# Score products of dilation 16 read their stationary operand from tiles in residue order

## The chip, the cores and the metric

One NeuronCore of one Trainium2 chip runs the whole program. The time is the device time of one launch in microseconds. The kernel before takes 3086.87 us (median of three runs, 3085.54 to 3091.45).

## The reference

One layer of an encoder on 2048 tokens of width 1024. Two groups of heads run on the same input: eight heads of dilated attention (64 wide) and four heads of a bidirectional mLSTM (128 wide); then an output projection, a gated feed-forward network with a convolution, and a small gated addition. The change touches the attention heads. For each head:

```python
ATTN_PATTERNS = ((128, 1), (512, 4), (2048, 16))      # window, dilation
def dilated_branch(q, k, v, dil, n_side):
    M = S // dil
    def to_res(t):
        return t.reshape(B, H, M, dil, hd).transpose(0, 1, 3, 2, 4)
    o, lse = banded_attention(to_res(q), to_res(k), to_res(v), n_side)
    ...
for window, dil in ATTN_PATTERNS:
    o, l = dilated_branch(q, k, v, dil, (window // 2) // dil)
    outs.append(o)
    lses.append(l)
wts = jax.nn.softmax(jnp.stack(lses, axis=0), axis=0)
out = jnp.sum(wts[..., None] * jnp.stack(outs, axis=0), axis=0)
```

Dilation 16 splits the 2048 tokens into 16 residue classes of 128 tokens, and each token attends within its class. Dilation 4 has four classes of 512 tokens in bands, dilation 1 is a band of tokens in their own order.

## The kernel before, in words

All matrix products of the layer run on TensorE; fp32 operands of the scores are held as a high part and a low part in fp32r, and a score block is two products added in PSUM.

**Layouts.** A head has its keys and queries with the features on the partitions and the 2048 tokens along the free axis. `qs` (queries, high part on partitions 0 to 63, low part on 64 to 127), `ks1` (keys, high part twice) and `ks2` (keys, low part, and a row 64 of ones) come from DRAM in token order (`load`, L858). `km1`, `km2` and `qm1`, `qm2` are the same in residue order: token 16a + r stands at place 128r + a. ACT makes `km1` and DVE makes `km2`, a quarter at a time (`keys_by_residue`, L879); DVE makes `qm1` (`queries_by_residue`, L887), and a DMA copies its upper half to `qm2`. Row 64 of `km2` is zero. Row 64 of `qm2` receives the negative row maximum, through DRAM.

**The two passes.** Pass A (`pass_a`, L936) multiplies queries (stationary) by keys (moving) for all three patterns; DVE takes the row maxima from PSUM (L956). At its end the three maxima are transposed, sent through DRAM, combined, and written to `qm2`. Pass B (`pass_b`, L1046) multiplies keys (stationary) by queries (moving), with the maximum subtracted by the extra row; ACT takes the exponential (L993), GpSimd (POOL) masks the band (L929, L931; DVE in half of the last head's steps), and the products with the values, fp32, follow three steps later (`values`, L1004), added into `oacc` by ACT (dilation 16) or DVE (the others).

**Units.** A pattern has 16 units (`unit`, L895). A unit is one stationary block of 128 tokens and one moving window, read from the tiles in residue order. The stationary block of dilation 1 is 128 neighbouring tokens of a tile in token order, that of dilation 4 every fourth token, that of dilation 16 every sixteenth: `return slice(i, i + 2033, 16), ...`. The moving window of dilation 16 is 128 neighbouring places of a tile in residue order; that of the others has 192 or 256 places.

**Steps and order.** A step of dilation 16 holds four units (eight products), a step of the others two units (four products). Pass A of a head has 21 steps: dilation 16 (4 steps), 1 (8), 4 (8), and the one that combines the maxima. Pass B has 20 score steps, dilation 16 (4), 4 (8), 1 (8), and three that only finish values. `run` (L1079) interleaves: one step of pass B of head h, then one step of the stream of A passes, which is 30 steps ahead at the start (`LEAD`). So beside the first three B steps of a head stand A steps 10 to 12 of the next head, beside B steps 4 to 11 its A steps 13 to 20, beside step 12 its step 21, and beside B steps 13 to 21 the A steps 1 to 9 of the head after it. `stream` (L1082) puts the loads and copies at yields of the A pass: the load of the next head at yield 8, query copies at 9, 11, 13 and 15, key copies of the next head at 14, 16, 18 and 20. Pass A of head 0 and the start of head 1's run beside the last of the input projections (L147 to L149).

**Memory.** The large tiles are pages of a pool of 22 (`NPAGES`), one page each for `qs`, `ks1`, `ks2`, `km1`, `km2`, `qm1`, `qm2`, `oacc` and the three value tiles `vt`. `qs`, `km1` and `km2` are given up at the end of pass A. PSUM has three banks for pass A (`psa`), three for pass B (`psb`), two for values (`pso`).

**Order of the instructions.** Each engine runs its own queue in order. A list scheduler fills the queues: it takes what is ready by priority in program order, and a tile waits until a page is free, so a DMA can be issued ahead of its place in the program. All DMAs of this part go through the queue of SyncE (SP), in order.

Of the kernel before, what the change touches and what calls it, by code (L numbers as in the profile page):

```python
# [11 lines left out]
F32 = mybir.dt.float32  # L12
# [8 lines left out]
P = 128  # L21
# [6 lines left out]
AH = 8  # L28
HD = 64
# [76 lines left out]
def page(g, shape, dtype=F32, name="pg"):  # L106
    n = int(np.prod(shape[1:]))
    return shaped(g.pages.tile([P, PAGE], dtype, name=name, tag="pg")[:shape[0], :n], shape)
# [720 lines left out]
class Attention:  # L829


    def __init__(self, g, pool, psA):
        nc = g.nc
# [34 lines left out]
        def residues(t):  # L868
            return t.rearrange("p (r a) -> p r a", a=P)
# [17 lines left out]
        def queries_by_residue(H, q):  # L887
            if q == 0:
                H.qm1 = page(g, [P, S], F32R, name="qm1")
                H.qm2 = page(g, [65, S], F32R, name="qm2")  # L890
            to_residues(nc.vector, H.qm1, H.qs, q)
            if q == 3:
                nc.sync.dma_start(H.qm2[:64].bitcast(F32), H.qm1[:64].bitcast(F32))

        def unit(p, i):  # L895

            if p == 0:
                lo, hi = max(0, 8 * i - 4), min(P, 8 * i + 12)
                return slice(P * i, P * i + P), (lambda t: residues(t)[:, :, lo:hi]), lo, hi, lo - (8 * i - 4)
            if p == 1:  # L900
                r, j = divmod(i, 4)
                lo, hi = max(0, 32 * j - 16), min(P, 32 * j + 48)
                t0 = r + 512 * j
                return slice(t0, t0 + 509, 4), (lambda t: t.rearrange("p (b r a) -> p r b a", r=4, a=P)[:, r, :, lo:hi]), lo, hi, lo - (32 * j - 16)
            return slice(i, i + 2033, 16), (lambda t: t[:, P * i:P * i + P]), 0, P, 0

        def width(p, lo, hi):
            return OUTER[p] * (hi - lo)
# [1 line left out]
        def shape3(p, ap, lo, hi):  # L910
            return ap if p == 2 else ap.rearrange("p (x y) -> p x y", y=hi - lo)
# [24 lines left out]
        def pass_a(h, H):  # L936

            mst = pool.tile([P, 3, 16], F32, name="mst", tag="mst", bufs=2)
            for p in (2, 0, 1):
                per = 4 if p == 2 else 2  # L940
                W = 512 // per
                for i0 in range(0, 16, per):
                    ps = psA.tile([P, 512], F32, name="psa", tag="psa")
                    for u in range(per):
                        st, win, lo, hi, off = unit(p, i0 + u)
                        o = shape3(p, ps[:, u * W:u * W + width(p, lo, hi)], lo, hi)
                        nc.tensor.matmul(o, lhsT=H.qs[:, st], rhs=win(H.km1), start=True, stop=False)  # L947
                        nc.tensor.matmul(o, lhsT=H.qs[:65, st], rhs=win(H.km2), start=False, stop=True)  # L948
                    for u in range(per):
                        i = i0 + u  # L950
                        st, win, lo, hi, off = unit(p, i)
                        n = width(p, lo, hi)
                        o = shape3(p, ps[:, u * W:u * W + n], lo, hi)
                        junk = pool.tile([P, 256], BF16, name="junk", tag="junk", bufs=1)
                        m = add[p] if p == 2 else add[p][:, :, off:off + hi - lo]
                        nc.vector.tensor_tensor_reduce(shape3(p, junk[:, :n], lo, hi), o, m, 1.0, -3e38, ALU.add, ALU.max, mst[:, p, i:i + 1])  # L956
                    yield
            ps = psA.tile([P, 512], F32, name="psa", tag="psa")
            for p in range(3):
                nc.tensor.transpose(ps[:16, P * p:P * p + P], mst[:, p], g.ident)  # L960
            neg = pool.tile([16, 2, P], F32, name="neg", tag="neg", bufs=1)
            nc.vector.tensor_scalar(neg[:, 0].rearrange("b (r a) -> b r a", r=16), ps[:16, 0:P].rearrange("b (a r) -> b r a", r=16), -1.0, None, ALU.mult)
            nc.vector.tensor_scalar(neg[:, 1].rearrange("b (r a) -> b r a", r=4), ps[:16, P:2 * P].rearrange("b (a r) -> b r a", r=4), -1.0, None, ALU.mult)
            nc.sync.dma_start(g.mx[h, 0].rearrange("r (b a) -> b r a", a=8), neg[:, 0].rearrange("b (r a) -> b r a", r=16))
            for r in range(4):
                nc.sync.dma_start(g.mx[h, 1].rearrange("(b r) (j a) -> r j b a", r=4, a=32)[r], neg[4 * r:4 * r + 4, 1].rearrange("j (b a) -> j b a", b=4))
            x12 = pool.tile([16, 2, P], F32, name="x12", tag="x12", bufs=1)
            nc.sync.dma_start(x12, g.mx[h].rearrange("s r a -> r s a"))
            nc.vector.tensor_tensor(x12[:, 0], x12[:, 0], x12[:, 1], ALU.min)
            mrow = pool.tile([16, P], F32R, name="mrow", tag="mrow", bufs=1)  # L970
            nc.vector.scalar_tensor_tensor(mrow, ps[:16, 2 * P:3 * P], -1.0, x12[:, 0], ALU.mult, ALU.min)
            nc.sync.dma_start(H.qm2[64:65].bitcast(F32).rearrange("o (r a) -> o r a", a=P), mrow.bitcast(F32))
            yield

        def weights(h, H, p, i0):

            per = 4 if p == 2 else 2
            W = 512 // per
            ps = self.psB.tile([P, 512], F32, name="psb", tag="psb")
            if i0 % (2 * per) == 0:  # L980
                H.e2 = raw(g, [P, 2, 512], name="e")
            e = H.e2[:, (i0 // per) % 2]
            us = [unit(p, i0 + u) for u in range(per)]
            widths = [width(p, x[2], x[3]) for x in us]
            for u in range(per):
                st, win, lo, hi, off = us[u]
                o = shape3(p, ps[:, u * W:u * W + widths[u]], lo, hi)
                nc.tensor.matmul(o, lhsT=H.ks1[:, st], rhs=win(H.qm1), start=True, stop=False)
                nc.tensor.matmul(o, lhsT=H.ks2[:, st], rhs=win(H.qm2), start=False, stop=True)  # L989
            for u0, u1 in ([(0, per)] if min(widths) == W else [(u, u + 1) for u in range(per)]):  # L990
                cs = slice(u0 * W, (u1 - 1) * W + widths[u0])
                st, win, lo, hi, off = us[u0]
                nc.scalar.activation(e[:, cs], ps[:, cs], AF.Exp, scale=0.125)  # L993
                if on_dve(h, p, i0 // per):
                    v = e[:, cs] if p == 2 else e[:, cs].rearrange("k (u x y) -> k u x y", u=u1 - u0, x=OUTER[p])
                    for u in range(u1 - u0):
                        if p == 2:
                            o, m = e[:, W * u:W * u + W], add[p]
                        else:
                            o, m = v[:, u], add[p][:, :, off:off + hi - lo]  # L1000
                        nc.vector.scalar_tensor_tensor(o, m, 0.0, o, ALU.is_equal, ALU.mult)
                else:
                    sel(p, e[:, cs], u1 - u0, hi - lo, off)
            return e, us, widths  # L1004
# [41 lines left out]
        def pass_b(h, H):  # L1046
            H.oacc = page(g, [P, S], F32, name="oacc")
            H.banks = {}
            steps = [(2, i) for i in range(0, 16, 4)] + [(p, i) for p in (1, 0) for i in range(0, 16, 2)]
            pend = []  # L1050
            for k, (p, i0) in enumerate(steps):
                pend.append((p, i0, weights(h, H, p, i0)))
                if len(pend) > LOOK:
                    values(h, H, *pend.pop(0))
                yield
            for x in pend:
                values(h, H, *x)
                yield
# [22 lines left out]
        def stream():  # L1081
            for q in range(4):  # L1082
                keys_by_residue(heads[0], q)
            for h in range(AH):
                H = heads[h]
                n = 0
                for _ in pass_a(h, H):
                    n += 1
                    if n == 8 and h + 1 < AH:
                        heads[h + 1] = load(h + 1)  # L1090
                    if n in (9, 11, 13, 15):
                        queries_by_residue(H, (n - 9) // 2)
                    if n in (14, 16, 18, 20) and h + 1 < AH:
                        keys_by_residue(heads[h + 1], (n - 14) // 2)
                    yield
                H.qs = H.km1 = H.km2 = None

        def start():
            heads[0] = load(0)
# [1242 lines left out]
```

## Time and profile before

| | us |
|---|---|
| median of three runs | 3086.87 |
| the profiled execution | 3087.83 |
| its span, first to last instruction | 3086.0 |
| PE busy (matmuls) | 2910.5 (94%) |
| PEld busy (weight loads) | 2481.0 (80%) |
| DVE busy | 2048.7 (66%) |
| ACT busy | 1277.4 (41%) |
| POOL busy | 1072.4 (35%) |

The attention heads run from about 617 to 1100 us of the span. Matmul durations overlap, since matmuls are pipelined: how fast TensorE works is read from the distance between starts. PE is the row of matmuls, PEld that of weight loads, which run ahead of their matmuls. The granted clock is a share of TensorE's full 2.4 GHz.

### The profile page before, as it was taken

To read this page: it belongs to the slowest core of one execution; us is meant where nothing else is said; L and a number is where in the kernel's file an instruction comes from. 1 tells how busy PE (TensorE), PEld (TensorE's weight loads), DVE (VectorE), ACT (ScalarE), POOL (GpSimd) and SP (SyncE) were. 2 spreads that over 40 slices of the span, in tenths; PEclk is the share of its full clock that TensorE was granted. 3 is DMA by queue.
4 is the path that set the end of the run, shared out by engine and by line. 5 is a ranking of instruction groups with operands and counts; after the bars stand their busy time and mean duration, and the time that the engine had idled before them with its cause. 6 is when DMAs were issued, how large, how long until landed. Compare 5 with 4: busy or idle time off the path is not lost.

```text
span 3086.0 us, 41017 instructions
## 1 busy us (share of the span) xinstructions
PE 2910.5 (94%) x14474; PEld 2481.0 (80%) x14474; DVE 2048.7 (66%) x4107; ACT 1277.4 (41%) x2428; POOL 1072.4 (35%) x1146
## 2 busy tenths in 40 slices
PE   8889899899999989799899999799999999999999
PEld 7867887799999978687578887678888777877887
DVE  5866786566656478534977777977777566646444
ACT  5555465433332346323444444444444223223332
POOL 2133423414444546101433332533334141433221
PEclk9999999879899899899899999899999999999999
DMA  7744425464452563556222223222224876765111
GB/s 216 206 137 130 142 95 171 135 159 98 97 122 59 157 202 122 156 166 224 95 82 82 82 78 103 79 82 82 82 82 138 299 266 226 238 211 203 45 43 43
DMA packets 386781, 419.70 MB, mean 136 GB/s; under 512 B 107448, under 2 KB 300856, under 8 KB 380936
## 3 DMA queue, kind: packets, MB, share of 16 engines
q1 hardware_dynamic: 386576, 417.09, 44.4%
q8 instruction: 114, 1.87, 0.3%
q14 instruction: 91, 0.75, 0.1%
HBM read 308.09 MB, written 104.61 MB: 134 GB/s over the span
## 4 chain that ended last, share of the span: by engine, by line
PE 44%; DVE 7%; DMA 5%; POOL 3%; issue 3%; ACT 1%; SPq 1%; POOLq 0%; DVEq 0%; ACTq 0%
PE ps L1806 8%; PE ps L1808 8%; PE ps L1807 8%; PE ps L149 6%; PE ps L147 6%; PE ps L148 5%; DMA ar<-a_d 2%; POOL ar L175 1%; DVE as L176 1%; DVE fw L176 1%; DMA wdr<-in_w_ffn_down_dram 1%; DVE wd L176 1%; DVE bl L176 1%; DVE wdr L175 1%; PE psm L1475 1%
## 5 line engine op out<-in xcount | busy, mean ns | idle before, releaser
L1806 PE MATMUL ps<-bh,fw 128*128 128x512 f32 x1232 | 494.6, 402 | 29.8 <-ACT fw L176 12.0
L1808 PE MATMUL ps<-bh,fw 128*128 128x512 f32 x1232 | 490.8, 399 | 7.5 <-DVE fw L176 7.5
L1807 PE MATMUL ps<-bl,fw 128*128 128x512 f32 x1232 | 491.8, 399 | 4.1 <-DVE bl L176 3.2
L175 POOL TENSOR_TENSOR sum<-fraw 128x512 f32<-128x512 f32 x132 | 197.1, 1493 | 405.9 <-DVE fw L176 359.8
L1806 PEld LDWEIGHTS ps<-bh,fw 128*128 128x128 f32 x1232 | 235.9, 191 | 94.3 <-ACT fw L176 14.2
L1808 PEld LDWEIGHTS ps<-bh,fw 128*128 128x128 f32 x1232 | 235.7, 191 | 64.1 <-DVE fw L176 10.4
L1807 PEld LDWEIGHTS ps<-bl,fw 128*128 128x128 f32 x1232 | 235.9, 191 | 60.5 <-DVE bl L176 7.4
L147 PE MATMUL ps<-wd,as 128*128 128x512 f32 x616 | 244.8, 397 | 14.1 <-ACT as L176 14.1
L149 PE MATMUL ps<-wd,as 128*128 128x512 f32 x616 | 245.4, 398 | 5.9 <-DVE as L176 5.9
L175 POOL TENSOR_TENSOR ar<-ar 128x768 f32<-128x768 f32 x80 | 143.3, 1811 | 294.6 <-DMA ar<-a_d 227.5
L148 PE MATMUL ps<-wd,as 128*128 128x512 f32 x616 | 243.4, 395 | 0.0
L176 ACT ACTIVATE fw<-sum 128x512 fp32r<-128x512 f32 x220 | 134.6, 628 | 241.3 <-DVE sum L175 142.5
L176 DVE TENSOR_TENSOR fw<-sum,fw 128x512 fp32r<-128x512 f32 x220 | 214.1, 988 | 8.0 <-ACT fw L176 7.7
L993 ACT ACTIVATE e<-psb 128x512 f32<-128x512 f32 (+2 forms) x240 | 95.5, 434 | 258.7 <-PE psb L989 248.5
L176 ACT ACTIVATE as<-ar 128x768 fp32r<-128x768 f32 x108 | 85.1, 792 | 271.7 <-POOL ar L175 218.7
L929 POOL TENSOR_SCALAR_AFFINE_SELECT e<-e 128x64 f32<-128x64 f32 (+2 forms) x225 | 98.4, 437 | 245.3 <-ACT e L993 238.7
L176 DVE TENSOR_TENSOR as<-ar,as 128x768 fp32r<-128x768 f32 x108 | 110.3, 1029 | 109.6 <-ACT as L176 109.3
L956 DVE CUSTOM_DVE_ANT_0 junk<-psa,mask 128x256 bf16<-128x256 f32 (+1 forms) x304 | 111.1, 365 | 86.8 <-PE psa L948 78.7
L1879 POOL TENSOR_TENSOR act<-act,up 128x512 f32<-128x512 f32 x88 | 129.2, 1468 | 87.9 <-DVE up L1828 68.8
L947 PE MATMUL psa<-km,qs 128*128 128x256 f32 (+2 forms) x384 | 150.4, 397 | 4.8 <-ACT km L875 4.8
L147 PEld LDWEIGHTS ps<-wd,as 128*128 128x128 f32 x616 | 117.0, 190 | 42.2 <-ACT as L176 16.6
L1870 DVE SCALAR_TENSOR_TENSOR act<-ext,fcw,act 128x512 f32<-128x512 f32 (+1 forms) x176 | 136.4, 815 | 16.7 <-ACT act L1868 16.1
(351 smaller groups left out, 7829.7 us busy)
## 6 DMA issues: line engine op xcount, KB each, us to landing
ar<-a_d SPq DMA_DIRECT2D x94, 384.0 KB
ar<-a_d SPq DMA_DIRECT2D x94, 320.0 KB
wdr<-in_w_ffn_down_dram SPq DMA_DIRECT2D x50, 512.0 KB
fraw<-in_w_ffn_gate_dram SPq DMA_DIRECT2D x22, 1024.0 KB
fraw<-in_w_ffn_up_dram SPq DMA_DIRECT2D x22, 1024.0 KB
a_d<-act SPq DMA_DIRECT2D x88, 256.0 KB
xT_d<-xT SPq DMA_DIRECT2D x32, 512.0 KB
bx<-xT_d SPq DMA_DIRECT2D x16, 1024.0 KB
```

Of the source, the lines that this page charges most:

```text
L147: g.nc.tensor.matmul(out, lhsT=sh, rhs=mh, start=start, stop=False)
L148: g.nc.tensor.matmul(out, lhsT=sh, rhs=ml, start=False, stop=False)
L149: g.nc.tensor.matmul(out, lhsT=sl, rhs=mh, start=False, stop=stop)
L175: eng[0].tensor_tensor(src, a, b, ALU.add if sign > 0 else ALU.subtract)
L176: return (lambda: g.nc.scalar.activation(hi, src, AF.Copy)), (lambda: eng[1].tensor_tensor(lo, src, hi.bitcast(F32), ALU.subtract))
L947: nc.tensor.matmul(o, lhsT=H.qs[:, st], rhs=win(H.km1), start=True, stop=False)
L956: nc.vector.tensor_tensor_reduce(shape3(p, junk[:, :n], lo, hi), o, m, 1.0, -3e38, ALU.add, ALU.max, mst[:, p, i:i + 1])
L1806: nc.tensor.matmul(ps, lhsT=w[:, 0, k], rhs=h[:, k], start=start and k == 0, stop=False, skip_group_check=True)
L1807: nc.tensor.matmul(ps, lhsT=w[:, 0, k], rhs=l[:, k], start=False, stop=False, skip_group_check=True)
L1808: nc.tensor.matmul(ps, lhsT=w[:, 1, k], rhs=h[:, k], start=False, stop=k == 3, skip_group_check=True)
L1870: nc.vector.scalar_tensor_tensor(act, ext[a][:, lo + k:hi + k], self.cw[:, k, f:f + 1], act, ALU.mult, ALU.add)
L1879: nc.gpsimd.tensor_tensor(act, act, up[a][:, lo:hi], ALU.mult)
```

## The change

Units of dilation 16 take their stationary block from the tile in residue order, where its 128 tokens are neighbours: `qm1` in place of `qs` in pass A, `km1` and `km2` in place of `ks1` and `ks2` in pass B. For that

- `unit` returns a function that cuts the block out of a tile, in place of a slice;
- pass A takes the patterns in the order of dilation 1, 4, 16, and its query copies come two yields earlier (7, 9, 11, 13), the load of the next head two yields later (10);
- `km1` and `km2` are kept until the fourth step of pass B, and at the end of pass A a DMA writes the row of ones into row 64 of `km2`, which pass A needs as zeros.

```diff
@@ unit
             if p == 0:
...
-                return slice(P * i, P * i + P), (lambda t: residues(t)[:, :, lo:hi]), lo, hi, lo - (8 * i - 4)
+                return (lambda t: t[:, P * i:P * i + P]), (lambda t: residues(t)[:, :, lo:hi]), lo, hi, lo - (8 * i - 4)
             if p == 1:
...
-                return slice(t0, t0 + 509, 4), (lambda t: t.rearrange("p (b r a) -> p r b a", r=4, a=P)[:, r, :, lo:hi]), lo, hi, lo - (32 * j - 16)
-            return slice(i, i + 2033, 16), (lambda t: t[:, P * i:P * i + P]), 0, P, 0
+                return (lambda t: t[:, t0:t0 + 509:4]), (lambda t: t.rearrange("p (b r a) -> p r b a", r=4, a=P)[:, r, :, lo:hi]), lo, hi, lo - (32 * j - 16)
+            return (lambda t: t[:, P * i:P * i + P]), (lambda t: t[:, P * i:P * i + P]), 0, P, 0
@@ pass_a
-            for p in (2, 0, 1):
+            for p in (0, 1, 2):
...
-                        nc.tensor.matmul(o, lhsT=H.qs[:, st], rhs=win(H.km1), start=True, stop=False)
-                        nc.tensor.matmul(o, lhsT=H.qs[:65, st], rhs=win(H.km2), start=False, stop=True)
+                        q = st(H.qm1 if p == 2 else H.qs)
+                        nc.tensor.matmul(o, lhsT=q, rhs=win(H.km1), start=True, stop=False)
+                        nc.tensor.matmul(o, lhsT=q[:65], rhs=win(H.km2), start=False, stop=True)
...
             nc.sync.dma_start(H.qm2[64:65].bitcast(F32).rearrange("o (r a) -> o r a", a=P), mrow.bitcast(F32))
+            nc.sync.dma_start(H.km2[64:65].bitcast(F32), g.kl[h, HD:HD + 1])
@@ weights
-                nc.tensor.matmul(o, lhsT=H.ks1[:, st], rhs=win(H.qm1), start=True, stop=False)
-                nc.tensor.matmul(o, lhsT=H.ks2[:, st], rhs=win(H.qm2), start=False, stop=True)
+                nc.tensor.matmul(o, lhsT=st(H.km1 if p == 2 else H.ks1), rhs=win(H.qm1), start=True, stop=False)
+                nc.tensor.matmul(o, lhsT=st(H.km2 if p == 2 else H.ks2), rhs=win(H.qm2), start=False, stop=True)
@@ pass_b
                 pend.append((p, i0, weights(h, H, p, i0)))
+                if p == 2 and i0 == 12:
+                    H.km1 = H.km2 = None
@@ stream
-                    if n == 8 and h + 1 < AH:
+                    if n == 10 and h + 1 < AH:
                         heads[h + 1] = load(h + 1)
-                    if n in (9, 11, 13, 15):
-                        queries_by_residue(H, (n - 9) // 2)
+                    if n in (7, 9, 11, 13):
+                        queries_by_residue(H, (n - 7) // 2)
...
-                H.qs = H.km1 = H.km2 = None
+                H.qs = None
```

## Rows read from the trace of the kernel before

**Rows 1.** The page, part 1: busy time, share of the span, instructions.
```profile
PE 2910.5 (94%) x14474; PEld 2481.0 (80%) x14474; DVE 2048.7 (66%) x4107; ACT 1277.4 (41%) x2428; POOL 1072.4 (35%) x1146
```

**Rows 2.** Busy time by stretch, one head: length, engines, clock, DMA share, GB/s.
```profile
779.00:833.70 54.70, 54.70 (x306) 53.82 (x304) 33.45 (x119) 17.88 (x38) 25.16 (x61) 0.94 0.49 108
```

**Rows 3.** Waits in that head: engine, line, releaser, total us, times, longest.
```profile
ACT e L993 <- PE psb L989: 35.4, 18, 5.8
DVE junk L956 <- PE psa L948: 16.1, 15, 1.7
```

**Rows 4.** Timeline of PE, an A step: start us, us, engine, line, tiles.
```profile
757.23 0.42 PE L947 MATMUL psa<-km,qs 128*128 128x128 f32 x1
...
758.80 0.39 PE L948 MATMUL psa<-km,qs 65*128 65x128 f32 x1
759.02 0.34 PE L988 MATMUL psb<-qm,ks 128*128 128x256 f32 x1
...
759.56 0.92 PE L1034 MATMUL pso<-e,vt 128*128 128x192 f32 x4
```

**Rows 5.** Timeline of PE, a B step of dilation 16.
```profile
726.28 0.33 PE L988 MATMUL psb<-qm,ks 128*128 128x128 f32 x1
...
727.99 0.34 PE L947 MATMUL psa<-km,qs 128*128 128x256 f32 x1
```

**Rows 6.** Timeline of PEld, values loads, then an A step of dilation 4.
```profile
739.14 0.99 PEld L1014 LDWEIGHTS pso<-e,vt 128*128 128x128 f32 x8
740.05 0.31 PEld L947 LDWEIGHTS psa<-km,qs 128*128 128x128 f32 x1
...
740.97 0.33 PEld L988 LDWEIGHTS psb<-qm,ks 128*128 128x128 f32 x1
```

**Rows 7.** Timeline of PE, products of dilation 1 with 192 columns.
```profile
719.20 0.25 PE L988 MATMUL psb<-qm,ks 128*128 128x192 f32 x1
719.29 0.28 PE L989 MATMUL psb<-qm,ks 65*128 65x192 f32 x1
719.40 0.35 PE L1034 MATMUL pso<-e,vt 128*128 128x64 f32 x2
```

**Rows 8.** Busy time by stretch, around the first B steps of head 1.
```profile
724.20:729.10 4.90, 4.90 (x28) 4.90 (x28) 1.91 (x7) 1.19 (x2) 1.04 (x3) 1.00 0.49 109
729.10:735.90 6.80, 6.80 (x32) 6.80 (x33) 4.26 (x12) 2.17 (x4) 4.45 (x7) 0.50 0.32 75
```

**Rows 9.** Busy time by stretch, pass B of head 7.
```profile
1055.00:1092.00 37.00, 32.83 (x180) 29.84 (x180) 21.47 (x47) 16.30 (x46) 17.07 (x32) 0.88 0.25 54
```

**Rows 10.** Busy time by stretch, the start of head 0.
```profile
616.50:633.50 17.00, 15.81 (x70) 15.53 (x71) 10.83 (x51) 7.13 (x10) 0.58 (x1) 0.50 0.93 209
```

**Rows 11.** Timeline of all engines, the start of head 0.
```profile
616.58 3.97 ACT L875 ACTIVATE km<-ks 128x512 fp32r<-128x512 f32 x4 [7.55 <-DMA ks<-qk_d]
617.69 0.48 PE L947 MATMUL psa<-km,qs 128*128 128x128 f32 x1 [4.80 <-ACT km L875]
...
619.85 2.20 DVE L877 CAST km<-ks 64x512 fp32r<-64x512 f32 x4
...
621.97 0.31 PE L948 MATMUL psa<-km,qs 65*128 65x128 f32 x1
```

**Rows 12.** Timeline of SP's queue: loads of head 4, maxima of head 2.
```profile
741.10 0.55 SPq L863 DMA_DIRECT2D qs<-qk_d  x1
...
758.93 1.38 SPq L865 DMA_DIRECT2D ks<-kl_d  x1
...
767.89 0.56 SPq L972 DMA_DIRECT2D qm<-mrow  x1
```

**Rows 13.** Timeline of DVE and ACT: key copies of head 4.
```profile
786.88 2.83 DVE L877 CAST km<-ks 64x512 fp32r<-64x512 f32 x2
790.13 4.07 ACT L875 ACTIVATE km<-ks 128x512 fp32r<-128x512 f32 x4
```

**Rows 14.** Busy time by stretch, the highest DMA rate.
```profile
600.00:620.00 20.00, 15.20 (x117) 14.71 (x115) 8.77 (x27) 7.84 (x17) 9.43 (x12) 0.91 0.95 229
```

## The prediction

> **What bounds the kernel now.** I read the page's busy shares first: the TensorE matmuls (PE) cover 94% of the span, its weight loads 80%, DVE 66% [rows 1]. The change touches attention alone, so the shares of that stretch count. In one full head of the steady state (779.0 to 833.7 us) PE is busy for all 54.70 us, DVE for 33.45, ACT for 17.88, POOL for 25.16 [rows 2]. The waits of that head name only engines that wait for PE: ACT 35.4 us, DVE 16.1 us; no wait of PE is listed [rows 3]. So PE's own instruction spacing is the period of a head, and I read that spacing from the starts in the timeline, not from the durations, which overlap.
>
> In an A step of dilation 16 (eight products of 128 columns) the starts run from 757.23 to 758.80, and the next line starts at 759.02: 1.79 us, or 0.22 us per product. The four products after it, of 256 columns each with a contiguous stationary operand, take from 759.02 to 759.56, 0.135 us each [rows 4]. Twice the columns in less time: the 0.22 us is not set by the moving columns. A B step of dilation 16 is the same: 726.28 to 727.99, 1.71 us [rows 5]. What the two have in common is the stationary operand, read at every 16th element.
>
> **What a contiguous load would cost.** No row shows a 128-column fp32r product with a contiguous stationary operand, so I bound it. Eight weight loads of 128 contiguous columns for 128 moving columns (the values products) run from 739.14 to 740.05: 0.114 us each [rows 6]. Score products with 192 columns and a contiguous operand start at 719.20, 719.29 and are followed at 719.40: 0.09 and 0.11 us [rows 7]. From below 0.09, from above 0.22 (no gain). I take 0.11, nearest to both rows: 0.88 us for a step of eight, a gain of 0.91 us in an A step and 0.83 us in a B step. At 0.09 a step would gain another 0.16 us.
>
> The Trainium skill ("TensorE: Matmul & The Clock Gate", LDWEIGHTS) says that a weight load takes its columns divided by 1.2, in ns, and nothing else: 107 ns for 128. The contiguous loads agree with it (0.114 us), the loads of dilation 16 do not (0.22 us). By that rule alone an order in memory changes nothing, and the time stays; that is the fourth case below.
>
> **The change, part by part.**
>
> *A steps, heads 1 to 7.* 7 x 4 steps at 0.91 us: 25.5 us less. All of it lies on PE, which sets the period [rows 2].
>
> *B steps, heads 0 to 6.* 28 steps at 0.83 us would be 23.2 us. But the granted clock is 1.00 up to 729.1 us and 0.50 (1.2 instead of 2.4 GHz) from 729.1 to 735.9 [rows 8]. The fall comes 4.9 us after the first B step of the head, in the stretch where no values products run yet. At half clock a contiguous product doubles to about 0.22 us, and gains nothing. In the changed order the first B steps stand beside A steps of dilation 4, 0.92 us each (740.05 to 740.97) [rows 6]; a pair is then 0.88 + 0.92 = 1.80 us, so 2.7 of the four B steps come ahead of the fall, and 1.3 gain nothing. 7 x 2.7 x 0.83 = 15.7 us less. Whether the clock still falls no row can tell, since the stretch gets shorter (three pairs of 1.80 instead of 2.25 us) and denser; I keep the fall here and make its absence a rival.
>
> *B steps, head 7.* Here the scan of the other mixer runs alongside and PE is busy for only 32.83 of 37.00 us [rows 9]. Between nothing and 4 x 0.83 = 3.3 us less; I take half, 1.7.
>
> *A pass of head 0.* It begins at 617.7 us, and the clock is at 0.50 from 616.5 to 633.5 [rows 10]. Now its dilation-16 steps stand in that stretch; after the change its dilation-1 steps do, which double there (8 steps of four products, 0.11 us more each: 3.5 us), while the dilation-16 steps move out of it and gain 4 x 0.91 = 3.6. The two cancel; 0, bounds plus and minus 3.
>
> *The order of the A pass.* The first step of dilation 16 needs a quarter of the keys in residue order, a step of dilation 1 needs all of them. Later heads have them early. In head 0 ACT's four copies run from 616.58 for 3.97 us, and PE, idle before, takes its first product at 617.69; DVE's four end near 622, and PE's first L948 product already waits until 621.97 [rows 11]. So at most 620.55 - 617.69 = 2.9 us more, at least 0 if projection products are placed ahead; I take 1.5 us more.
>
> *Queries earlier, load later.* The casts of the queries are the same, two steps sooner: nothing on PE. The five loads of the next head move from yield 8 to yield 10 of an A pass, its key copies stay at yields 14 to 20. In the trace the loads of head 4 are issued from 741.10 to 758.93 us, its first key casts run at 786.88 (DVE) and 790.13 (ACT) [rows 12, 13]: 28 us of cover, of which the shift and the pages held longer take a part. Nothing as long as it lasts; the price without it is in the slower case.
>
> *Keys held longer, row of ones.* km1 and km2 stay in their two pages of 22 until the fourth B step, some 15 steps more. One more DMA per head of a row of 8 KB goes on SP's queue behind the maximum row (767.89 us for head 2) [rows 12], and is read by the first B step, 11 us later (779). The maximum row itself waits longer than the products that the new DMA waits for, so nothing new waits, and what is queued behind it (a chunk of the values load) moves by its 0.56 us of issue. 0.
>
> The sum: 25.5 + 15.7 + 1.7 - 1.5 = 41.4 us. The profiled execution took 3087.8 us (span 3086.0 and 1.8 around it), 0.9 above the median of the three, 3086.9. So 3087.8 - 41.4 = 3046.4, and against the median 3045.
>
> What is late next: with 6 us less per head, DVE stands at 33.45 of some 49 us, and still waits for PE.
>
> **The rivals.**
>
> 1. *The clock no longer falls* in the denser stretch. For it: the dilation-16 stretch is the only one of a head in which it falls. Against it: three steps without values products remain. Then the 1.3 steps of seven heads gain too (7.6 us), and the half-clock time itself goes: the eight values products of a step double in it from 0.91 us [rows 6], and some score products with them, so about 1.2 us per head, 8.5 us. 3045 - 16 = 3029.
>
> 2. *Another engine takes over for part of the head.* DVE's and ACT's order near the first B steps is dense, since the key copies of the head after next (2.83 us on DVE, 4.07 us on ACT [rows 13]) and the output product fall there; faster steps bring them nearer. If half the gain is lost: 3066. Against it: both engines idle for over a third of the head [rows 2].
>
> 3. *Slower: pages and late loads.* The loads of a head come only when three pages are free. With km1 and km2 held and the load at yield 10, four steps (some 8 us) are left to the key copies, if the loads are not issued ahead of their place as they are now. A head's five loads are 2.5 MB; the best rate of a stretch, 229 GB/s [rows 14], makes that 11 us, the mean of a head, 108 GB/s [rows 2], makes it 23 us. ACT and DVE would stand in front of the copies for 3 to 15 us and the exponentials behind them with them. The point from which it decides is 41.4 / 6 = 7 us of PE standing still in each of six heads; at 10 us the time would be 3045 + 60 = 3105. Against it: 28 us of cover now.
>
> 4. *It does nothing.* If the 0.22 us belongs to products of 128 fp32r columns and not to the stride, the steps stay as they are: 3087. For it: no contiguous one is in the trace. Against it: 128 columns in the values products at 0.114 us.
>
> **How the numbers follow.** The forecast has 0.47 (own range 3036 to 3052: the spacing of 0.09 us gives 0.16 x 47 = 7.5 us more, head 0 plus or minus 3, its start 1.5, head 7 1.7). The clock case 0.28, the partly covered one 0.13, no effect 0.06, slower 0.06. A measurement of this kernel tells about 0.2%, 6 us, from no change; so faster 0.88, same 0.06, slower 0.06. For eight in ten I leave out the last two, the worse part of the covered case, and the best of the clock case with 0.09 us: 3022 to 3067.
>
> **What would show it.** In the timeline of the changed kernel the dilation-16 products should start 0.11 us apart, both in A and B steps, and a head should take some 49 us, with PE busy throughout. The clock at half for 7 to 10 us per head, about 5 us after the first B step, is the forecast; a full clock there is rival 1. Waits of PE for ACT or DVE in the B steps of dilation 4, with a DMA of the keys behind them, are rival 3. Products at 0.22 us with contiguous operands are rival 4. The prediction is wrong if the spacing stays above 0.15 us, or if a head's period shrinks by less than 3 us.

## The result, and the profile after

The changed kernel takes 3058.49 us (median of four runs, 3050.90 to 3060.52), the kernel before in the same rounds 3088.36 (3085.54 to 3091.45). The ratio is 0.9899, 95% interval 0.9878 to 0.9919: about 30 us, or 1%, faster. The time lies in the forecast's range (3022 to 3067), but 13.5 us above the forecast itself and outside its own range (3036 to 3052). The profiled execution is one of the longer ones, 3060.42 us.

Most lines of the code move by two to five: what was L947 and L948 is now L949 and L950, L988 and L989 are L991 and L992, L956 is L958.

The page's line of busy times answers to [rows 1]:

```profile
PE 2875.3 (94%) x14474; PEld 2437.7 (80%) x14474; DVE 2032.9 (66%) x4107; ACT 1278.4 (42%) x2428; POOL 1084.5 (35%) x1146
```

PE is 35.2 us shorter with the same 14474 instructions. Busy time by stretch (columns as in [rows 2]): one steady head, then the stretch around its first B steps, then the rest up to the end of the last head:

```profile
770.88:820.35 49.47, 49.47 (x305) 48.47 (x304) 31.59 (x119) 17.91 (x38) 26.81 (x61) 0.93 0.54 119
769.00:773.90 4.90, 4.90 (x34) 4.82 (x32) 2.17 (x8) 1.20 (x2) 1.25 (x4) 1.00 0.49 109
773.90:780.70 6.80, 6.80 (x33) 6.80 (x32) 3.56 (x11) 2.27 (x4) 3.30 (x6) 0.50 0.56 130
1024.79:1061.60 36.81, 32.77 (x179) 29.56 (x178) 20.18 (x44) 13.80 (x39) 15.93 (x31) 0.91 0.23 50
```

A head is 49.47 us long where it was 54.70 [rows 2], and PE is still busy for all of it. The clock still falls to 0.50 for 6.80 us [rows 8], here 4.1 us after the first B step begins (769.78). Over heads 1 to 6 that distance is 4.1 to 5.9 us, and it was 4.1 to 6.4 before; in head 1 of [rows 8] the first B step begins at 723.96, so the fall came 5.1 us after it, not the 4.9 that the prediction reads. In that same head PE waits for nobody; the list of waits answers to [rows 3]:

```profile
ACT e L996 <- PE psb L992: 30.1, 18, 5.5
...
DVE junk L958 <- PE psa L950: 10.3, 12, 1.5
```

The timeline of PE, a B step of dilation 16 ahead of the fall of the clock, and one after it [rows 5]:

```profile
771.73 0.24 PE L991 MATMUL psb<-qm,km 128*128 128x128 f32 x1
771.81 0.27 PE L992 MATMUL psb<-qm,km 65*128 65x128 f32 x1
...
772.59 0.43 PE L949 MATMUL psa<-km,qs 128*128 128x192 f32 x1
...
775.92 0.36 PE L991 MATMUL psb<-qm,km 128*128 128x128 f32 x1
...
777.57 0.73 PE L1017 MATMUL pso<-e,vt 128*128 128x128 f32 x2
```

Eight products take 772.59 - 771.73 = 0.86 us, where they took 1.71; after the fall 777.57 - 775.92 = 1.65, a gain of next to nothing. And an A step, answering to [rows 4]:

```profile
790.08 0.41 PE L949 MATMUL psa<-km,qm 128*128 128x128 f32 x1
...
790.88 0.28 PE L949 MATMUL psa<-km,qm 128*128 128x128 f32 x1
791.00 0.28 PE L950 MATMUL psa<-km,qm 65*128 65x128 f32 x1
791.11 0.43 PE L991 MATMUL psb<-qm,ks 128*128 128x192 f32 x1
```

The starts are 0.11 us apart (791.00 to 791.11), but the step takes 1.03 us, not 0.88: its second product starts 0.25 us after the first (790.33). Summed from each start to the next over all heads, the A products of dilation 16 went from 56.96 to 32.27 us, the B products from 55.02 to 37.12: 42.6 us together.

Two things were given back. The first is waits of PE, at the start of head 0 and at the transposes of the maxima (L962), in heads 0 and 7:

```profile
620.86 1.01 PE L949 MATMUL psa<-km,qs 128*128 128x192 f32 x3 [6.11 <-ACT km L875]
...
655.93 0.38 PE L962 MATMUL psa<-ident,mst 128*16 128x128 f32 x1 [3.50 <-DVE mst L958]
...
1000.66 0.28 PE L962 MATMUL psa<-ident,mst 128*16 128x128 f32 x1 [1.97 <-DVE mst L958]
```

The first was 4.80 us before [rows 11], the other two were not there. All waits of PE from 616 us to the end of the last head sum to 17.3 us, where they were 9.3: 8.0 us more. So the last head ends at 1061.6 instead of 1096.8 us, 35.2 us earlier. The second is no part of the change: from there to the end the program is the same, yet took 1997.0 us in this profile and 1989.2 in that of before.

The loads have less cover. The last load of head 4 in SP's queue, and the first key cast on DVE, with the last key cast and the query casts:

```profile
764.87 0.34 SPq L865 DMA_DIRECT2D ks<-kl_d  x1
```

```profile
776.91 0.60 DVE L877 CAST km<-ks 64x512 fp32r<-64x512 f32 x1
...
785.37 0.63 DVE L877 CAST km<-ks 64x512 fp32r<-64x512 f32 x1
785.91 2.22 DVE L877 CAST qm<-qs 128x512 fp32r<-128x512 f32 x4
```

776.91 - 764.87 = 12 us, where it was 28 [rows 12, 13].

### The profile page after: what moved, and what is told of

The parts are those of the page before. It is cut to its first block, busy times and chain, and to the rows that moved or that the text cites. A ratio compares the mean times of both kernels' runs of the same rounds, so it can differ in the third digit from the quotient of the medians.

```text
span 3058.6 us, 41026 instructions
## 1 busy us (share of the span) xinstructions
PE 2875.3 (94%) x14474; PEld 2437.7 (80%) x14474; DVE 2032.9 (66%) x4107; ACT 1278.4 (42%) x2428; POOL 1084.5 (35%) x1146
## 4 chain that ended last, share of the span: by engine, by line
PE 46%; DVE 7%; DMA 5%; issue 3%; POOL 3%; ACT 1%; SPq 1%; POOLq 0%; DVEq 0%; ACTq 0%
PE ps L1811 8%; PE ps L1812 8%; PE ps L1813 8%; PE ps L149 6%; PE ps L147 6%; PE ps L148 6%; DMA ar<-a_d 2%; POOL ar L175 1%; DVE fw L176 1%; DVE as L176 1%; DMA wdr<-in_w_ffn_down_dram 1%; PE psm L1480 1%; PE psm L1481 1%; PE psm L1389 1%; DVE bl L176 1%
## 5 line engine op out<-in xcount | busy, mean ns | idle before, releaser
L958 DVE CUSTOM_DVE_ANT_0 junk<-psa,mask 128x256 bf16<-128x256 f32 (+1 forms) x304 | 111.7, 367 | 71.9 <-PE psa L950 62.4
L147 PEld LDWEIGHTS ps<-wd,as 128*128 128x128 f32 x616 | 117.4, 191 | 42.9 <-ACT as L176 16.9
L149 PEld LDWEIGHTS ps<-wd,as 128*128 128x128 f32 x616 | 117.3, 190 | 38.8 <-DVE as L176 12.1
```

The source lines that it names most:

```text
L147: g.nc.tensor.matmul(out, lhsT=sh, rhs=mh, start=start, stop=False)
L149: g.nc.tensor.matmul(out, lhsT=sl, rhs=mh, start=False, stop=stop)
```

## The experiments

Each is a small edit of the changed kernel, timed beside the kernel before (3088.3 to 3088.8 us).

**The three parts alone.** First, pass A alone reads the tiles in residue order; pass B keeps the strided block:

```diff
-lhsT=st(H.km1 if p == 2 else H.ks1)
+lhsT=H.ks1[:, i0 + u:i0 + u + 2033:16] if p == 2 else st(H.ks1)
(ks2 the same)
```

> Only pass A reads its dilation-16 stationary blocks from the tile in residue order; pass B reads them at every 16th element as before; order, loads, pages and the new DMA are as in the changed kernel. Theory (the stride of the weight load sets the spacing): pass A's 256 products of dilation 16 stay at about 32 us of PE, pass B's go back from 37 to 55 us, so about 18 us slower than the changed kernel, 3076. Rival (the new order of pass A and of the loads brings the gain, not the operand): no slower than the changed kernel, 3058.

Second, pass B alone (in pass A the query block is `H.qs[:, i0 + u:i0 + u + 2033:16]`):

> Only pass B reads its dilation-16 blocks from the tiles in residue order; pass A reads them at every 16th element, in the new order. Theory: pass A's products go back from 32 to 57 us, but the waits of the maximum transposes for the row maxima (5.5 us in the changed kernel) go, since PE's steps of dilation 16 are again slower than DVE's: 19 to 25 us slower than the changed kernel, 3078 to 3084. Rival (order): 3058.

Third, both blocks strided, so that only the order, the times of loads and copies, the held pages and the row of ones are left of the change:

> Both passes read the dilation-16 blocks at every 16th element, all else as in the changed kernel. Theory: the kernel before plus the dearer start of head 0 (1 to 3 us): 3088 to 3092. Rival 1 (the order itself gains): 3070 or less. Rival 2 (the order and the pages held longer cost as much as the missing part of the forecast, 8 us or more): 3096 or more.

Measured: A alone 3073.45 us (ratio 0.9952, 0.9938 to 0.9966), B alone 3070.31 (0.9942, 0.9929 to 0.9955), order alone 3092.05 (1.0010, 0.9999 to 1.0022). The first and the third came as the theory said; B alone is 8 us faster than its range. Against the order alone, A is worth 18.6 us, B 21.7, and both 33.6. The sum of the parts, 40.3, is more than the whole. Part of that is the clock: with B alone the B products of dilation 16 take 34.7 us, in the changed kernel 37.1, and attention runs at half clock for 78.5 us instead of 88.7. So the operand's order in memory makes the gain, and the order of the steps costs a little or nothing. With A alone PE waits 5.06 us at L962; with B alone that wait is gone: it needs the faster A steps, which now stand last.

**Is it the stride of 16, or any stride?** In dilation 4 the stationary block is replaced by 128 neighbouring tokens. These are the wrong tokens: this kernel computes other scores and is only a probe of time.

```diff
-return (lambda t: t[:, t0:t0 + 509:4]), ...
+return (lambda t: t[:, P * i:P * i + P]), ...
```

> The changed kernel with the stationary blocks of dilation 4 taken as 128 neighbouring tokens, so these are the wrong tokens and the outputs of that pattern are not the reference's; the same number and shape of instructions. Theory (every stride in the weight load costs, not only 16): the 512 products of dilation 4, now 0.25 us each (129 us of PE in all), go to about 0.125 us; 64 us less on PE, of which at least 40 show: 2995 to 3018. Rival (only products of 128 columns gain, since with 192 and 256 columns the columns are the limit): 3058.

Measured: 3044.38 us, but scattered from 3025.61 to 3060.89 (ratio 0.9856, 0.9820 to 0.9891): neither expectation. The profile is of the fastest run. The timeline of PE, an A step of dilation 4:

```profile
803.70 0.33 PE L949 MATMUL psa<-km,qs 128*128 128x256 f32 x1
...
804.09 0.27 PE L950 MATMUL psa<-km,qs 65*128 65x192 f32 x1
804.20 0.25 PE L991 MATMUL psb<-qm,km 128*128 128x128 f32 x1
```

Four products take 0.50 us (0.49 to 0.55 over the steps at full clock); strided, in the changed kernel, they take 0.96 to 1.03. So a stride of 4 elements costs about as much per product, 0.12 us, as one of 16, 0.10 us. And since the block comes from the same tile `qs` in both cases, it is the stride that costs, not the tile. The Trainium skill ("SBUF — State Buffer", the note on cachelines) says that consecutive reads are at full bandwidth only within a line of 16 bytes. Four fp32 are such a line, so either stride leaves it at each element; the nearly equal cost agrees. By the rule of the columns alone, the fourth case of the prediction, neither step should have changed; the measurement decides.

In this profile attention ends 29 us earlier than in the changed kernel, less than half of the 64 us that the theory counts on PE. Other engines came into the way, as the waits of PE up to the end of the last head show (total, times, longest):

```profile
PE pso L1017 <- ACT oacc L1018: 18.7, 6, 5.7
...
PE psa L962 <- DVE mst L958: 11.0, 4, 4.4
```

and, from the same list, what ACT and DVE stood for:

```profile
ACT e L996 <- DVE att L1080: 22.3, 6, 6.1
...
DVE att L1080 <- DMA zb<-zr_d: 18.8, 6, 4.4
```

ACT stands behind DVE, and DVE behind the DMA of the normalizers. This is where rival 2 sets in: at 43.9 to 47.8 us per steady head, not at 49.5.

**Is the wait at L962 from the order?** Pass A in the order 1, 16, 4, with the query copies at yields 1, 3, 5 and 7:

```diff
-for p in (0, 1, 2):
+for p in (0, 2, 1):
...
-if n in (7, 9, 11, 13):
+if n in (1, 3, 5, 7):
```

> The changed kernel with pass A in the order of dilation 1, 16, 4 and its query copies at yields 1, 3, 5, 7; the operands are the same. Theory (the transposes of the maxima wait because the four reductions of a dilation-16 step take DVE longer than PE's 0.9 us step, and these steps now stand right in front): with dilation 4 in front the waits of PE for the row maxima go from 5.5 us to 1 us or less, so the end of attention comes some 4 us sooner; 3052 to 3056, at the limit of what can be told from the time, so the waits and the start of the last head's division decide. Rival (they wait for the loads that DVE's queue holds, whatever stands in front): the 5.5 us stay, 3058.

Measured: 3054.87 us (3051.48 to 3061.30; 0.9893, 0.9877 to 0.9909), no different from the changed kernel. The waits at L962 are gone, 5.5 us to 0, but others of 2.5 us came (L950 for DVE, L1017 for ACT), and the last head ends at 1063.4 us, not earlier. Together with B alone this shows that the wait needs fast steps of dilation 16 right ahead of the transposes. The query copies moved too, so how much of the wait was theirs is not separated; a gain in time is not shown.

**Dilation 4 of pass A in earnest.** ACT copies the queries into one more page in the order of four classes, and the A steps of dilation 4 take their block from it:

```diff
+def queries_by_four(H, q): H.qf = page(...); ACT copies a quarter of H.qs
-q = st(H.qm1 if p == 2 else H.qs)
+q = H.qf[:, P * (i0 + u):P * (i0 + u) + P] if p == 1 else st(H.qm1 if p == 2 else H.qs)
...
+if n in (1, 3, 5, 7): queries_by_four(H, (n - 1) // 2)
+if n in (2, 4, 6, 8): queries_by_residue(H, (n - 2) // 2)
```

> The changed kernel with one more tile: ACT copies the queries into the order of four residue classes (four copies per head, in place of the page of the token-order queries, which is given up after yield 8), and pass A takes its dilation-4 stationary blocks from it, contiguous. Query copies by 16 at yields 2, 4, 6, 8. Theory (stride 4 costs as much as stride 16): pass A's 256 products of dilation 4 go from 63 to about 32 us; less some 5 us of waits for ACT and DVE near the division, as the probe showed: 3030 to 3038. Rival (another engine covers it: ACT gets 4.3 us more per head, and PE waits for it): 3050 or more.

The same with a constant of the scheduler raised (`Z2` from 6 to 9):

> The kernel with contiguous dilation-4 queries, and the division by the denominators put three steps of pass B later (step 9 in place of 6). Theory (in the faster kernels DVE, in order, waits for the broadcast of the denominators, and ACT and PE behind it): these waits go, 3 to 12 us less than without it: 3022 to 3032. Rival (the division only moves to a denser place, or holds its buffers longer so that the exponentials wait): no less, or 3 to 6 us more.

Measured: 3074.32 us (0.9965, 0.9950 to 0.9979) and 3075.01 (0.9957, 0.9942 to 0.9973): slower than the changed kernel by 16, so both theories failed, and the later division brought nothing. The products themselves did gain, as in the probe: the eight A steps of dilation 4 take 4.2 us in a steady head, where they took 8.0. The queue of SP, and the two casts that stand for the loads, in the first of them:

```profile
780.02 0.56 SPq L865 DMA_DIRECT2D ks<-kl_d  x1
```

```profile
789.20 0.58 DVE L877 CAST km<-ks 64x512 fp32r<-64x512 f32 x1 [3.77 <-DMA ks<-kl_d]
```

```profile
786.81 2.97 ACT L875 ACTIVATE km<-ks 128x512 fp32r<-128x512 f32 x3 [4.87 <-DMA ks<-qk_d]
```

The last load of head 4 goes out at 780.02, not at 764.87. DVE and ACT stand still in front of the key casts, and the maxima behind them come late: PE waits 4.10 us for DVE (790.18). This is the path of rival 3. What makes the load late is not separated: this kernel holds one page more up to yield 8, but it also takes the pages of the copies by 16 five yields earlier. The kernel with the order 1, 16, 4 takes them six yields earlier and holds no extra page. Counted from the first B step of head 2, the load goes out 4.9 us ahead of it in the changed kernel, 2.8 behind it there and 4.9 behind it here.

**Does more time for the loads mend it?** The key copies of that kernel at yields 17 to 20:

```diff
-if n in (14, 16, 18, 20) and h + 1 < AH:
+if n in (17, 18, 19, 20) and h + 1 < AH:
```

> The kernel with the extra tile of queries in order of four classes (74 us of it went into waits of DVE and ACT for late key loads and what stood behind them), with one thing changed: the copies of the next head's keys stand at yields 17, 18, 19 and 20 in place of 14, 16, 18 and 20, so the loads have three yields more, some 6 us, where the casts stood still for 3.8 us (DVE) and 4.9 us (ACT). Theory (the late loads are the price): the waits of the casts for the key DMAs go, and with them PE's waits for maxima and exponentials; the dilation-4 gain of pass A, 7 heads x 8 steps x 0.4 us = 22 us in part, shows: 3030 to 3050 us, below the changed kernel's 3058. Rival (the DVE and ACT work itself is too dense, or the first steps of dilation 1 now wait for the last key copies): the waits move to DVE's and ACT's casts or to the first A steps, and the time stays at 3065 us or above.

Measured: 3086.84 us (0.9998, 0.9986 to 1.0010): the rival. The waits for key DMAs are gone, and other waits came. In the head from 773.60 to 827.74 us:

```profile
DVE att L1086 <- DMA zb<-zr_d: 4.8, 1, 4.8
...
ACT e L1002 <- DVE att L1086: 4.6, 1, 4.6
PEld pso L1043 <- POOL e L938: 4.2, 2, 3.0
PE pso L1043 <- POOL e L938: 3.6, 2, 2.6
```

**How near was rival 3 in the changed kernel?** Its load moved four yields on, and nothing else:

```diff
-if n == 10 and h + 1 < AH:
+if n == 14 and h + 1 < AH:
```

> The changed kernel with the load of the next head at yield 14 in place of 10, right ahead of the first key copy. In the changed kernel the last load of head 4 is issued at 764.87 us and the first key cast runs at 776.90, 12 us of cover (before: 758.93 and 786.88, 28 us). Theory (the place of the load in the program sets when it goes out): four yields are some 9 us, the cover is down to 3 us, about the time that the load takes, ACT and DVE begin to wait for key DMAs for 1 to 5 us per head, and the time is 3065 to 3095 us. Rival (free pages set it, since loads go out ahead of their place): the loads go out as before and the time stays within 6 us of the changed kernel, 3052 to 3064 us.

Measured: 3094.30 us (1.0016, 1.0005 to 1.0028). The whole gain is gone, as the theory's number said, but not through the wait that it named: no cast waits for a DMA in the list of that head. The casts themselves come later. Here are DVE, then PE:

```profile
811.33 0.72 DVE L877 CAST qm<-qs 128x512 fp32r<-128x512 f32 x1
...
812.74 1.95 DVE L877 CAST km<-ks 64x512 fp32r<-64x512 f32 x3
...
815.64 0.68 DVE L877 CAST km<-ks 64x512 fp32r<-64x512 f32 x1
...
817.99 0.29 DVE L958 CUSTOM_DVE_ANT_0 junk<-psa,mask 128x128 bf16<-128x128 f32 x1
```

```profile
818.35 0.38 PE L962 MATMUL psa<-ident,mst 128*16 128x128 f32 x1 [4.59 <-DVE mst L958]
818.52 1.70 PE L1037 MATMUL pso<-e,vt 128*128 128x256 f32 x4
...
824.52 0.76 PE L1037 MATMUL pso<-e,vt 128*128 128x256 f32 x3
```

In the changed kernel the key casts lie in the dilation-4 steps (776.91 to 786), where DVE has slack. Here they lie between the last maxima of dilation 16, which PE awaits at L962, and so do four query casts, behind the division L1080 (3.90 us from 807.37). The last load of head 4 went out at 794.30, 18 us ahead of the first key cast, so the load itself was not late; why the list scheduler put the casts there is not shown. The busy times by stretch price it, head and stall:

```profile
783.28:839.97 56.69, 52.10 (x305) 50.66 (x304) 31.87 (x119) 18.09 (x38) 29.22 (x61) 0.88 0.49 104
817.00:823.80 6.80, 5.46 (x20) 5.10 (x21) 3.22 (x15) 0.60 (x1) 3.23 (x6) 0.51 0.29 61
```

The head is 56.69 - 49.47 = 7.2 us longer than in the changed kernel, of which 4.6 is the wait; the rest is the clock, which fell in the wait (0.51 in the stretch). Heads 1 to 5 all have such a wait of 4.5 to 4.7 us and are 6.3 to 7.2 us longer: a stall of PE here costs about one and a half times its length.

**The clock.** The steps in which it falls are those without values products. With the values two steps behind the scores instead of three:

```diff
-LOOK = 3
+LOOK = 2
```

> The changed kernel with the values products two steps behind the score products in place of three (LOOK = 2). In the changed kernel the clock falls to 0.50 in each steady head for 6.8 us, 3 us after the first B step of dilation 16 (771.73, fall at 773.9), in the three steps that have no values products beside them. Theory (what is missing there is the dense values products): one step less without them, the fall comes later or stays away, a head takes 1.7 to 3.4 us less, and the time is 3038 to 3050 us. Rival (the values products now come before their masks are ready: in the steps of dilation 1, 1.7 us apart, exponential and masks take some 3 us): PE waits for POOL at the values products, and the time is 3058 us or above. Second rival: the fall has nothing to do with the values products: it stays at 6.8 us per head and the time at 3052 to 3064 us.

Measured: 3057.35 us (0.9902, 0.9883 to 0.9921), no different from the changed kernel, as the second rival's number said. But its reason does not hold: in the dilation-16 steps of heads 2 to 6 the clock did not fall, and heads 2 to 5 take 47.1 to 48.0 us, such as:

```profile
825.99:873.97 47.98, 47.47 (x305) 46.10 (x304) 31.81 (x119) 17.75 (x38) 29.82 (x61) 1.00 0.57 123
```

That is the state of rival 1, worth 1.5 to 2.4 us a head in these four. Head 6 gained nothing: at 46.6 us it is as long as in the changed kernel, and its clock fell for 3.4 us behind a wait at L962. Two waits of PE took the rest back: 4.94 us for POOL in head 1, which is new, and 4.52 us for DVE in head 7, where the changed kernel waits 2.29. So two steps in heads 2 to 6 alone (`2 if 2 <= h <= 6 else LOOK`):

> The changed kernel with the values products two steps behind in heads 2 to 6 only, three steps in the others. With two steps in all heads the clock stayed at 1.00 in heads 2 to 6 and these took 47.1 to 48.0 us in place of 49.5, but two waits outside them took the gain back: 4.94 us at L1017 for POOL in head 1 (739.17) and 4.52 us at L1037 for DVE in head 7 (1039.88). Theory (those two waits belong to the shorter distance in heads 1 and 7): they go, 5 x 1.8 = 9 us remain, the attention ends some 9 us earlier than in the changed kernel, and the time is 3045 to 3053 us. Rival (the waits come from elsewhere, or the gain is taken by other stalls or by the rest of the kernel, whose length varies by 8 us from execution to execution): 3054 to 3064 us.

and in heads 0 to 6 (`2 if h <= 6 else LOOK`):

> The changed kernel with the values products two steps behind in heads 0 to 6, three steps in head 7. Up to head 6 its instructions are those of the kernel with two steps in all heads, where the clock stayed at 1.00 in heads 2 to 6 (47.1 to 48.0 us each); with two steps in heads 2 to 6 alone the same steps of a head saw the clock fall for 3.4 to 10.2 us (48.8 to 50.8 us each). Theory (what comes before decides it, so the same instructions give the same clock): no fall in heads 2 to 6 again, 47 to 48 us each, the wait of 4.5 us in head 7 gone, and 3048 to 3054 us. Rival (where the falls come differs from execution to execution and is not set by the instructions): falls of 3.4 to 10.2 us in several of heads 2 to 6, 49 to 51 us each, and 3053 to 3062 us.

Measured: 3048.63 us (3047.59 to 3051.63; 0.9872, 0.9855 to 0.9888), the shortest time of a kernel that computes the reference, though its interval overlaps that of the changed kernel; and 3065.73 us (3050.14 to 3074.34; 0.9913, 0.9888 to 0.9938). The first time is what the theory said, but by luck: the wait in head 1 is gone and the one in head 7 back at 2.3 us, but the clock fell again in each of heads 2 to 6. The second lies above both of its ranges; its clock falls, as the rival said. One head of the first:

```profile
817.30:867.94 50.64, 50.64 (x305) 49.73 (x304) 31.65 (x119) 18.10 (x38) 27.52 (x61) 0.90 0.52 117
```

and one head of the second, with a stretch in which its clock falls:

```profile
881.83:933.04 51.21, 50.90 (x305) 49.70 (x304) 31.67 (x119) 18.09 (x38) 28.49 (x61) 0.90 0.52 115
882.68:889.80 7.12, 7.12 (x39) 7.12 (x38) 2.49 (x14) 1.68 (x3) 2.08 (x6) 0.64 0.37 87
```

Up to head 7 its instructions come in the same order, on every engine, as in the kernel with two steps throughout, which saw a clock of 1.00 here. So what the values products beside these steps do to the clock is not settled: the same order of work saw both. In the profile of the 3048.63 us kernel the last head ends at 1058.8 us, only 2.8 earlier than in the changed kernel, and the unchanged rest took 1987.5 us, 9.5 less.

## Why the prediction was right, and where it was not

**What the gain is.** Right. The spacing is 0.11 us, in A and in B steps; PE stayed the bound of every steady head; the fourth rival (no effect) is out by the timeline, and the three kernels with the parts alone show that the operand's order does it.

**The terms of the sum.** In the profiled executions, in us saved:

| | forecast | measured |
|---|---|---|
| A products of dilation 16, heads 1 to 7 | 25.5 | 21.2 |
| B products of dilation 16, heads 0 to 6 | 15.7 | 14.5 |
| B products of dilation 16, head 7 | 1.7 | 3.4 |
| head 0, A products of dilation 16 and 1 | 0 | 3.3 |
| the start of head 0 | -1.5 | -1.3 |
| other waits of PE | 0 | -6.7 |
| all other products (the remainder) | 0 | 0.8 |
| attention | 41.4 | 35.2 |

The products together come out near the forecast (42.4 against 42.9), but by luck: the terms miss to both sides. An A step takes 0.98 to 1.03 us where 0.88 was taken, since its first product takes longer than 0.11. In head 0 the dilation-16 steps gained the 3.5 us that were foreseen, but the dilation-1 steps, which were to lose as much, lost 0.3. Head 7's B steps saw the full clock. That only part of the B steps gain was right, but not the same part everywhere. The fall comes 4.1 and 5.9 us after the first B step in turn, so two or three of the four steps lie ahead of it, and heads 1 to 6 gain 2.0 to 2.8 us each, 2.4 in the mean (forecast 2.2). Head 0's four steps lie at half clock, before and after, and gain 0.1 us.

**The clock case** (rival 1, 0.28) did not come: half-clock time in attention went from 95.6 to 88.7 us, and 6.8 us per head are left. Two steps of look-ahead showed it once, in four full heads, and its worth there, 1.5 to 2.4 us, is near the 2.3 that the rival's 16 us make over seven heads.

**The start of head 0.** Forecast 1.5 us later, bounds 0 and 2.9; the wait grew by 6.11 - 4.80 = 1.3.

**What was missed in attention** is the step on the order of the A pass. It asked only what the first steps of the new order need, not who waits for the last. With dilation 16 last, the maxima of a step that now takes 1.0 instead of 1.8 us stand directly ahead of the transposes. DVE's timeline ahead of the two waits, in head 0 and in head 7:

```profile
651.60 1.62 DVE L877 CAST qm<-qs 128x512 fp32r<-128x512 f32 x3
...
653.46 0.29 DVE L958 CUSTOM_DVE_ANT_0 junk<-psa,mask 128x128 bf16<-128x128 f32 x1
653.68 0.08 DVE L958 DVE_READ_ACCUMULATOR2_ANT mst<- 128x1 f32 x1
653.80 0.29 DVE L958 CUSTOM_DVE_ANT_0 junk<-psa,mask 128x128 bf16<-128x128 f32 x1
...
999.23 0.07 DVE L1400 MEMSET v<- 128x16 f32 x1 [2.62 <-DMA v<-vog_d]
```

The maxima stand 0.34 us apart, four to a step, 1.4 us of DVE for a step of 0.9 to 1.0 us on PE, so work in DVE's queue there becomes a wait of PE: 3.50 us in head 0, behind three query casts of 1.62 us and the eight maxima queued after them, and 1.97 us in head 7, where DVE waited 2.62 us for a DMA of the other mixer. With the start's 1.3 and 1.2 us of smaller waits this makes 8.0 us, where 1.5 were forecast. It is a small case of rival 2, in two heads whose A pass runs beside other work, the projections (head 0) and the other mixer (head 7); the forecast had looked only at a steady head [rows 2, 3].

**What was missed outside** is that the rest of the program keeps its time only on average. In the 14 profiles of this study it took 1987.3 to 1997.0 us, and the changed kernel's was the longest. The account of the profiled execution: 3046.4 forecast, 6.2 us more in attention (41.4 against 35.2), 7.8 more behind it: 3060.4. The clock goes with it: in that rest it was at 0.50 for 117.3 us in the changed kernel's profile and for 97.3 in that of before, and over the 14 profiles the rest is longer where that time is longer (correlation 0.78). What sets the clock there was not found out. Of the median's miss, this share can't be told for certain, since only one of the four runs has a profile.

**Rival 3** (slower) was priced right and nearer than its chance of 0.06 said. Four yields of the load decide it: 6.3 to 7.2 us per head, against a point of decision of 7. But its path there is another. The casts did not stand and wait for the loads; they ran later, into the place where PE needs DVE. Casts that wait for their loads came in the kernel with the extra page.

## What to carry to other kernels

Where TensorE sets the period, compare the spacing of products by their stationary operand: one read at a stride can cost twice its time, and a copy that is in memory already may serve in its place. When a step becomes faster, look at who waits for its last result, and at the stretches that run beside other work: there part of the gain was lost here. And expect a stall of TensorE to cost more than its length where the clock falls behind it.

## What the runs showed of the hardware

- A stationary operand read at a stride of 4 fp32 elements costs about as much per product as one at 16: at full clock, steps of four products take 0.96 to 1.03 us strided and 0.49 to 0.55 contiguous (dilation 4), steps of eight 1.71 to 1.79 and 0.84 to 1.03 (dilation 16).
- At half clock the stride costs nothing: 1.65 us per step contiguous in the changed kernel, 1.70 strided (731.17 to 732.87) in the kernel before. The strided step is no slower at 0.50 than at 1.00 (1.71); the contiguous one doubles.
- The same instructions in the same order saw the clock stay at 1.00 in heads 2 to 5 of one execution and fall for 3.4 to 20.5 us in each of heads 2 to 6 of another (two steps of look-ahead, throughout and up to head 6). The Trainium skill ("TensorE: Matmul & The Clock Gate", Part 1) says that how many products pass at a kernel's start before the clock rises differs from run to run of one kernel; here it is the falls that differ, in the middle of a kernel. The times of that last kernel scatter by 24 us.
